# A recurrent layer on one core: small products outside the scan are held back behind the weight products

## The chip, the cores and the metric

One NeuronCore of a Trainium2 chip runs the whole layer. The metric is device time in microseconds (us) of one execution. The engines are PE (TensorE, matrix products), DVE (VectorE), ACT (ScalarE), POOL (GpSimd) and SP (which issues DMAs). Each works through its own instruction list in order and waits on semaphores for the others.

## The reference, cut to what matters

One layer with a context stream of 256 tokens and a latent stream of 256, width 2048. After a modulated norm, one input projection feeds two branches: 16 RWKV-7 heads and 4 gated linear attention heads.

```python
p = h @ lp["w_in"]
...
def step(s, inp):
    w_t, k_t, v_t, a_t, b_t = inp[:5]
    sa = jnp.einsum("bhvk,bhk->bhv", s, a_t)
    s = s * w_t[:, :, None, :] + sa[..., None] * b_t[:, :, None, :] + v_t[..., None] * k_t[:, :, None, :]
    y = jnp.einsum("bhvk,bhk->bhv", s, inp[5]) if emit else None
...
mixed = (jax.nn.sigmoid(f["g_a"]) * (y_a.astype(dt) @ lp["w_a"])
         + jax.nn.sigmoid(f["g_b"]) * (y_b.astype(dt) @ lp["w_b"]))
return mixed @ lp["w_out"]
```

The RWKV recurrence runs in both directions, over the context first and then over the latent tokens.

## The kernel before, in words

The kernel orders its own instructions. While the program is built, class `Issue` (from line 67) keeps a clock for each engine from estimated costs. Every piece of work is a generator, a track, which yields lists of operations; `run` (line 255) takes the track that can start first by these clocks, and `emit` (line 146) writes its operations to the engines. So the order on each engine is fixed once, and the chip follows it, however long things take there. In this text "planner" is this class, and "planned" times are its estimates.

A track has a number for its priority; the smaller one goes first among those that can start within 40 ns of each other. Track 99, `stream` (line 612), issues the **weight products**: 128x128 blocks of `w_in`, `w_a`, `w_b` and `w_out` against 256 tokens, each as three products (high and low halves, `three`, line 637). They fill `acc`. Before, ACT casts the raw weights to `wH` and DVE takes the difference `wL` (`splitter`, line 596); one such half tile serves 12 weight products, and five can be ready at a time.

The recurrent stretch (from line 1651) works through eight blocks of two heads. For each block these tracks run, and all but the last have priorities of 3 or more:

- `fe_track` (line 979): products `pq`, `pw`, `pal`, and on DVE the features `kn`, `C`, `bk`, `kd`, `ar`.
- `bt_track` (1093): transposes `pbt` of `bk`. `ab_track` (1105): products `pab`. `gg_track` (1119): `pgc`, `pgl`. `mv_track` (1238): transposes `pV`. `bv_track` (1068): `pb`.
- `inv_track` (1168): inverts 64x64 triangular blocks. ACT copies `Lin`, DVE transposes it to `M`, POOL runs a recurrence of 60 operations on `M` and `tm`, DVE transposes `M` back to `Lin`, then PE does `pH` and `pZ`, and ACT and DVE copy the result to `Z`.
- `sc_track` (1256), priority 2: **the scan**, eight steps of `p` (in the code `p1`), `pU`, `pSs` and `pY`, with copies on ACT and DVE between them, and after the last step `pyt`. It needs `Z`, `BK` and `UV` of its block.

During this stretch the weight products are those of 48 column blocks of `w_in` (`add_cm`, line 645); when the last block's features are made, those of `w_b` and `w_a` may follow. After the scans come the rest of these and `w_out`.

The choice of the next operation on PE in `run`, before:

```python
same = [x for w, x in c if x[6] == tr[6] and w <= w0 + win]
best = min(same, key=lambda x: x[0]() if callable(x[0]) else x[0])
if tr[6] == "pe" and self.since > 1200:
    best = next((x for x in same if x[0] == 99), best)
if tr[6] == "pe" and best[0] != 99 and 0.6 and self.cooling():
    best = next((x for w, x in c if x[0] == 99 and w <= w0 + 150), best)
```

Here `c` holds the tracks that could go and the time at which each could, `x[0]` is the priority, `x[3]` the list of operations, `x[5]` the planned time at which its inputs are there, and `win` is 40 ns. So a small product goes as soon as the planner holds it for ready, after the weight product in hand; the second rule lets a weight product in after 1200 ns of small ones, the third where the planner fears for the clock of PE.

Of the kernel before, what the change touches and what calls it, by code (L numbers as in the profile page):

```python
# [76 lines left out]
class Issue:  # L77
# [12 lines left out]
    def __init__(self, ps, groups):  # L90
        self.t = dict.fromkeys(self.LAT, 0.0)
        self.at, self.rd, self.rings, self.free_at, self.tracks = {}, {}, {}, {}, []
        self.ps, self.groups = ps, groups
        self.bank_free, self.bank_of = {b: 0.0 for g in groups.values() for b in g}, {}
        self.busy, self.psum, self.kept = set(), set(), {}
        self.n = 0
        self.table = 0
        self.work = self.since = self.small = 0.0
        self.load_at = self.stream_at = 0.0
        self.corners, self.ticks = [], {}  # L100

# [153 lines left out]
    def run(self, done):  # L255
        while not done():
            best, c = None, []
            for tr in self.tracks:
                w = self.when(tr)
                if w is None:  # L260
                    continue
                if w < 0:
                    best = tr
                    break
                c.append((w, tr))
            if best is None:
                if not c:
                    raise RuntimeError("stuck: " + str([(t[4], t[2].gi_frame.f_lineno) for t in self.tracks]))
                w0, tr = min(c, key=lambda x: x[0])
                win = 40  # L270
                same = [x for w, x in c if x[6] == tr[6] and w <= w0 + win]
                best = min(same, key=lambda x: x[0]() if callable(x[0]) else x[0])
                if tr[6] == "pe" and self.since > 1200:
                    best = next((x for x in same if x[0] == 99), best)
                if tr[6] == "pe" and best[0] != 99 and 0.6 and self.cooling():
                    best = next((x for w, x in c if x[0] == 99 and w <= w0 + 150), best)
            g = best[3]
            send = None
            if isinstance(g, list):
                w0 = self.work  # L280
                for op in g:
                    self.emit(op)
                if best[0] == 99:
                    self.since = 0.0
                else:
                    self.since += self.work - w0
                    self.small += self.work - w0
            elif isinstance(g, Claim):
                send = self.take(g)
            self.step(best, send)  # L290
# [40 lines left out]
def hybrid_layer(tc, a, out):  # L331
    nc = tc.nc
    es = ExitStack()
    with es:
# [6 lines left out]
        iss = Issue(ps, {"acc": (0, 1, 2, 3), "pa": (4, 5, 6, 7), "gg": (4, 5, 6, 7), "st": (2,), "u1": (3,), "py": (4,),  # L341
                         "g3": (5, 6, 7), "o2": (2, 3),
                         "f4": (0, 1, 2, 3, 4, 5, 6), "s1": (7,), "s2": (6, 7),
                         "xp": (0, 1, 2, 3, 4, 5, 6, 7)})
# [1304 lines left out]


        state["b0"] = iss.small
        iss.groups["acc"] = (0, 1)
        xes, fes = ExitStack(), ExitStack()
        xp = Pool(iss, xes.enter_context(tc.tile_pool(name="rwx", bufs=1, reuse_waits="tile")))
# [157 lines left out]
```

## Time and profile before

| | us |
|---|---|
| median of 3 runs | 1364.46 (1361.43 to 1368.26) |
| the profiled execution, own time | 1361.36 |
| its span, first to last instruction | 1359.6 |
| PE busy in it | 1270.1 (93%) |
| DVE busy | 968.3 (71%) |
| ACT busy | 718.2 (53%) |
| POOL busy | 543.3 (40%) |

The profile is of one execution. "Busy" counts an engine as busy while any instruction is in flight on it. An idle time in square brackets behind an instruction names the operation whose end it waited for. Nearly all instructions carry the line of one helper (L304 before), so they are told apart by the names of their tiles. The recurrent stretch lies at about 595 to 1125 us of the span, the last of the scan and its evacuation end near 1172, and the rest of the span is weight products.

### The profile page before, as it was taken

Reading aid. Unit: us, or ns where it says so; the run is one execution under the profiler, and the core shown is the slowest. Engines: PE = TensorE matmul, PEld = TensorE weight load, DVE = VectorE, ACT = ScalarE, POOL = GpSimd, SP = SyncE. Lnnn points to the kernel's source line nnn. Section 1 sums busy time; section 2 is a strip of 40 time slices with the busy share of each in tenths; the row PEclk is TensorE's granted clock in tenths of the full one; section 3 lists DMA queues with packets and bytes.
Section 4 is the critical chain, followed back from the end, with each engine's and each line's share of the span. In section 5 each row is a group of like instructions: output and inputs, shape, how many; then the busy total and the mean of one; then the engine's idle time right before and its main releaser. Section 6 shows DMA issues by size and latency. Waiting matters only on the chain. (4 is left out here: it accounts for less than half of the span.)

```text
span 1359.6 us, 29662 instructions
## 1 busy us (share of the span) xinstructions
PE 1270.1 (93%) x11479; PEld 1068.1 (79%) x11479; DVE 968.3 (71%) x2031; ACT 718.2 (53%) x1449; POOL 543.3 (40%) x684
## 2 busy tenths in 40 slices
PE   5999999999999999999899999799989999999996
PEld 3555578688788897998777778677878888999876
DVE  4433497885965737767978998698978776668656
ACT  5222244343334444486577678667766666445443
POOL 0000476676570000005888729673983550000012
PEclk9999999999999999999889999799979999999999
DMA  9999465455462433576632443234433545789564
GB/s 347 354 340 311 132 195 168 150 171 160 145 202 79 134 102 97 153 196 171 157 85 76 113 118 92 77 99 114 108 78 94 138 105 145 203 247 271 185 230 144
DMA packets 311186, 220.45 MB, mean 162 GB/s; under 512 B 37354, under 2 KB 286724, under 8 KB 310532
## 3 DMA queue, kind: packets, MB, share of 16 engines
q1 hardware_dynamic: 311044, 218.55, 55.5%
q8 instruction: 90, 1.47, 0.4%
q14 instruction: 52, 0.43, 0.1%
HBM read 199.76 MB, written 12.46 MB: 156 GB/s over the span
## 5 line engine op out<-in xcount | busy, mean ns | idle before, releaser
L304 DVE TENSOR_TENSOR wL<-raw,wH 128x512 fp32r<-128x512 f32 x484 | 377.2, 786 | 170.2 <-ACT wH L304 165.0
L304 ACT CAST wH<-raw 128x512 fp32r<-128x512 f32 x484 | 295.1, 616 | 328.5 <-PE acc L304 208.7
L304 PE MATMUL acc<-lH,wH 128*128 128x256 f32 x896 | 285.1, 318 | 0.5 <-ACT tg L304 0.5
L304 PE MATMUL acc<-lL,wH 128*128 128x256 f32 x896 | 256.0, 286 | 0.0
L304 PE MATMUL acc<-lH,wL 128*128 128x256 f32 x896 | 255.6, 285 | 0.2 <-DVE wL L304 0.2
L304 PEld LDWEIGHTS acc<-lH,wH 128*128 128x128 f32 x896 | 173.4, 194 | 21.1 <-issue 4.5
L304 POOL TENSOR_TENSOR tm<-M 64x30 f32<-64x30 f32 (+14 forms) x240 | 160.1, 667 | 74.3 <-DVE M L304 48.1
L304 POOL TENSOR_TENSOR M<-M,tm 64x30 f32<-64x30 f32 (+14 forms) x240 | 170.1, 709 | 18.7
L304 PEld LDWEIGHTS acc<-lL,wH 128*128 128x128 f32 x896 | 174.5, 195 | 3.1 <-issue 1.7
L304 PEld LDWEIGHTS acc<-lH,wL 128*128 128x128 f32 x896 | 173.9, 194 | 0.4 <-DVE wL L304 0.4
L304 PE MATMUL acc<-hH,wH 128*128 128x512 f32 (+1 forms) x416 | 168.7, 406 | 1.3 <-ACT lo L304 1.3
L304 PE MATMUL acc<-hH,wL 128*128 128x512 f32 (+1 forms) x416 | 157.2, 378 | 0.0
L304 PE MATMUL acc<-hL,wH 128*128 128x512 f32 (+1 forms) x416 | 156.3, 376 | 0.1
L304 PEld LDWEIGHTS acc<-hH,wH 128*128 128x128 f32 x416 | 78.6, 189 | 38.1 <-issue 22.9
L304 POOL TENSOR_TENSOR xs<-yg,fg 128x512 f32<-128x512 f32 (+1 forms) x10 | 13.5, 1371 | 231.4 <-DVE yg L304 231.4
L304 POOL TENSOR_TENSOR gw<-gw,csl 128x512 f32<-128x512 f32 x60 | 71.1, 1185 | 61.9 <-DMA gw<-in_w_mod_dram 61.9
L304 PEld LDWEIGHTS acc<-hH,wL 128*128 128x128 f32 x416 | 78.4, 188 | 15.5 <-DVE wL L304 0.4
L304 POOL TENSOR_TENSOR ga<-ga,gw 128x512 f32<-128x512 f32 x60 | 88.6, 1476 | 4.2
L304 PEld LDWEIGHTS acc<-hL,wH 128*128 128x128 f32 x416 | 78.9, 190 | 10.6 <-DVE hL L304 0.4
L304 PE MATMUL acc<-yH,wH 128*128 128x256 f32 x256 | 73.0, 285 | 0.0
L304 PE MATMUL acc<-yL,wH 128*128 128x256 f32 x256 | 72.8, 284 | 0.0
L304 PE MATMUL acc<-yH,wL 128*128 128x256 f32 x256 | 72.8, 284 | 0.0
(318 smaller groups left out, 2627.7 us busy)
## 6 DMA issues: line engine op xcount, KB each, us to landing
raw<-in_w_in_dram SPq DMA_DIRECT2D x174, 512.0 KB, 4.0
wm<-in_w_mod_dram SPq DMA_DIRECT2D x64, 512.0 KB, 6.9
gw<-in_w_mod_dram SPq DMA_DIRECT2D x64, 256.0 KB, 4.0
raw<-in_w_out_dram SPq DMA_DIRECT2D x32, 512.0 KB, 4.8
raw<-in_w_b_dram SPq DMA_DIRECT2D x16, 512.0 KB, 4.1
raw<-in_w_a_dram SPq DMA_DIRECT2D x16, 512.0 KB, 4.9
kv<-kvo SPq DMA_DIRECT2D x16, 256.0 KB, 3.9
tg<-tg SPq DMA_DIRECT2D x32, 128.0 KB, 3.8
```

Source lines behind the costliest of these rows:

```text
L304: op = Op("dma" if name == "dma_start" else self.key, name, lambda: f(*a, **k), aps[0], aps[1:], func, k.get("accum_out"), any(x.tensor.na ...
```

## The change

A list of small products of a track other than the scan is no longer taken if the last thing on PE was a weight product, a weight product is ready within 40 ns, and the list has been ready for less than 2000 planned ns. A weight product goes in its place, and the list is looked at again each time. The hold ends when the 2000 ns are over, when no weight product is ready, or when some other product, in practice one of the scan, has been taken: `on99` is then false and the held lists follow it freely. The hold is switched on at the start of the recurrent stretch.

```diff
@@ class Issue, __init__
+        self.defer, self.on99 = 0.0, False
@@ Issue.run
                 if tr[6] == "pe" and self.since > 1200:
                     best = next((x for x in same if x[0] == 99), best)
+                if (tr[6] == "pe" and self.defer and self.on99 and best[0] != 99 and isinstance(best[3], list)
+                        and (best[0]() if callable(best[0]) else best[0]) > 2 and self.t["pe"] - best[5] < self.defer):
+                    best = next((x for w, x in c if x[0] == 99 and isinstance(x[3], list) and w <= w0 + win), best)
...
                 for op in g:
                     self.emit(op)
+                if g[0].key == "pe":
+                    self.on99 = best[0] == 99
@@ the start of the recurrent stretch
         state["b0"] = iss.small
+        iss.defer = 2000.0
```

No operation is added or removed; the order on the engines is another from the first transposes `pV` of the stretch on. Three places follow. First PE in the second block, from `pw` to the transposes `pbt` of `bk`. Before:

```order
L304 MATMUL pw<-low,wh 128x512
L304 MATMUL pw<-low,wlo 128x512
L304 MATMUL acc<-lH,wH 128x256
L304 MATMUL acc<-lL,wH 128x256
L304 MATMUL acc<-lH,wL 128x256
L304 MATMUL pbt<-ident,bk 128x128 x4
L304 MATMUL pal<-low,wh 128x512
L304 MATMUL pal<-low,wlo 128x512
L304 MATMUL pbt<-ident,bk 128x128 x4
```

The same place in the changed program:

```order
L310 MATMUL pw<-low,wh 128x512
L310 MATMUL pw<-low,wlo 128x512
L310 MATMUL acc<-lH,wH 128x256
L310 MATMUL acc<-lL,wH 128x256
L310 MATMUL acc<-lH,wL 128x256
...
L310 MATMUL pbt<-ident,bk 128x128 x4
L310 MATMUL pal<-low,wh 128x512
L310 MATMUL pal<-low,wlo 128x512
L310 MATMUL pbt<-ident,bk 128x128 x4
```

The three rows of weight products stand there seven times in a row: 21 weight products instead of 3 ahead of `pbt`. From `pq` of this block to this `pbt` there were 105 weight products and are now 156.

Second DVE at the same place, where `bk` is made, from the copies `Dt` to the second `bk`. Before:

```order
L304 COPY Dt<-eC 128x4 x2
L304 SCALAR_TENSOR_TENSOR bk<-t_7006,C 128x8x64
L304 TENSOR_TENSOR wL<-raw,wH 128x512
L304 TENSOR_TENSOR kd<-kc,ta 128x512
L304 TENSOR_TENSOR wL<-raw,wH 128x512
L304 SCALAR_TENSOR_TENSOR rc<-acc,vec,rc 128x3x63
L304 TENSOR_TENSOR bk<-kd,C 128x8x64
```

In the changed program:

```order
L310 COPY Dt<-eC 128x4 x2
L310 TENSOR_TENSOR wL<-raw,wH 128x512
L310 SCALAR_TENSOR_TENSOR rc<-acc,vec,rc 128x3x63
L310 SCALAR_TENSOR_TENSOR bk<-t_7123,C 128x8x64
L310 TENSOR_TENSOR wL<-raw,wH 128x512
L310 SCALAR_TENSOR_TENSOR rc<-acc,vec,rc 128x4x63
L310 TENSOR_TENSOR kd<-kc,ta 128x512
L310 TENSOR_TENSOR wL<-raw,wH 128x512
L310 SCALAR_TENSOR_TENSOR rc<-acc,vec,rc 128x4x63
L310 TENSOR_TENSOR wL<-raw,wH 128x512
L310 SCALAR_TENSOR_TENSOR rc<-acc,vec,rc 128x3x63
L310 TENSOR_TENSOR bk<-kd,C 128x8x64
```

From `kn` of this block to this second `bk` there were 6 splits `wL` and one operation on `rc`, and are now 9 and 6. Ahead of the first scan step as a whole DVE has 9 splits more than before.

Third PE at `pH` of the fourth block, which stands among the scan steps of the third. Before:

```order
L304 MATMUL pab<-ar,bk 64x64 x16
L304 MATMUL acc<-lH,wH 128x256
L304 MATMUL acc<-lL,wH 128x256
L304 MATMUL acc<-lH,wL 128x256
L304 MATMUL pSs<-UV,BK 64x64 x4
L304 MATMUL pY<-UV,GMr 64x64 x4
L304 MATMUL pH<-Lin,GMo 32x32 x16
```

In the changed program:

```order
L310 MATMUL acc<-lH,wH 128x256
L310 MATMUL acc<-lL,wH 128x256
L310 MATMUL acc<-lH,wL 128x256
...
L310 MATMUL pSs<-UV,BK 64x64 x4
L310 MATMUL pY<-UV,GMr 64x64 x4
L310 MATMUL pH<-Lin,GMo 32x32 x16
```

The weight products ahead of `pSs` stand there seven times again, 21 instead of 3, and `pab` of the next block has moved behind `pH`.

Over the whole program from the stretch on, PE's 3369 weight products lay in 266 unbroken runs and lie in 255 now. Up to the first scan step there were 573 of them and are 669 now; up to the last `pSs` 2073, now 2217; after it 1296, now 1152.

## Rows read from the trace of the kernel before

**Rows 1.** The page, engines: busy us, share of the span, instructions.

```profile
PE 1270.1 (93%) x11479; PEld 1068.1 (79%) x11479; DVE 968.3 (71%) x2031; ACT 718.2 (53%) x1449; POOL 543.3 (40%) x684
```

**Rows 2.** Stages: window and length, busy us (instructions) by engine, PE's clock, DMA.

```profile
595.00:1175.00 580.00, 536.69 (x6591) 466.24 (x6591) 472.10 (x999) 397.04 (x838) 346.91 (x509) 0.95 0.44 114
1175.00:1360.00 185.00, 172.01 (x1163) 158.59 (x1161) 121.85 (x216) 84.04 (x158) 13.54 (x10) 0.98 0.70 217
```

**Rows 3.** Waits of PE, 595 to 1175 us: total us, times, longest.

```profile
PE pH L304 <- DVE Lin L304: 9.6, 4, 6.9
PE p L304 <- DVE UV L304: 6.0, 13, 1.9
PE pSs L304 <- DVE UV L304: 3.9, 9, 1.0
PE pbt L304 <- DVE bk L304: 3.5, 1, 3.5
PE pbt L304 <- ACT BK L304: 3.0, 1, 3.0
...
PE pgl L304 <- ACT rs L304: 2.4, 1, 2.4
...
PE pq L304 <- ACT sz L304: 1.8, 1, 1.8
PE pgl L304 <- DVE Z L304: 1.8, 1, 1.8
PE pgl L304 <- DVE GMr L304: 1.4, 1, 1.4
...
PE pgl L304 <- DVE GM L304: 0.7, 1, 0.7
```

**Rows 4.** The chain that ended last: start us, length, what.

```profile
1172.27 84.60 PE acc L304 x705
```

**Rows 5.** Timeline of PE around `pab` of the first block: start us, length, instruction.

```profile
616.01 0.28 PE L304 MATMUL acc<-lH,wL 128*128 128x256 f32 x1
616.22 1.15 PE L304 MATMUL pab<-ar,bk 64*64 64x64 f32 x32
617.30 0.39 PE L304 MATMUL acc<-lH,wH 128*128 128x256 f32 x1
617.52 0.28 PE L304 MATMUL acc<-lL,wH 128*128 128x256 f32 x1
```

**Rows 6.** Timeline of DVE and PE at `pbt` of the second block.

```profile
645.35 1.15 DVE L304 TENSOR_TENSOR wL<-raw,wH 128x512 fp32r<-128x512 f32 x1
...
650.77 0.40 DVE L304 SCALAR_TENSOR_TENSOR rc<-acc,vec,rc 128x189 f32<-128x189 f32 x1
651.10 0.77 DVE L304 TENSOR_TENSOR bk<-kd,C 128x512 f32<-128x512 f32 x1
...
651.92 1.12 PE L304 MATMUL pbt<-ident,bk 128*128 128x128 f32 x4 [3.46 <-DVE bk L304]
```

**Rows 7.** Timeline of POOL and DVE ahead of `pH` of the fourth block.

```profile
857.31 0.25 POOL L304 TENSOR_TENSOR M<-M,tm 64x30 f32<-64x30 f32 x1
...
857.68 2.03 DVE L304 STREAM_TRANSPOSE Lin<-M 64x1024 f32<-64x1024 f32 x1 [5.61 <-POOL M L304]
```

**Rows 8.** Stages: POOL's recurrence of the first and of the last block.

```profile
625.50:674.30 48.80, 43.22 (x366) 40.83 (x367) 42.42 (x66) 28.16 (x48) 44.11 (x62) 0.93 0.58 151
1065.00:1107.70 42.70, 41.37 (x463) 35.65 (x463) 32.33 (x79) 26.19 (x70) 37.96 (x61) 1.00 0.56 143
```

**Rows 9.** Timeline of PE and DVE from `pZ` to `Z`, first block.

```profile
683.15 1.53 PE L304 MATMUL pZ<-Lin,GMo 32*32 32x32 f32 x48
...
687.93 0.69 DVE L304 COPY Z<-pZ 32x512 f32<-32x512 f32 x1 [0.65 <-ACT Z L304]
```

**Rows 10.** Timeline of PE just after the wait of rows 6.

```profile
654.76 0.41 PE L304 MATMUL acc<-lL,wH 128*128 128x256 f32 x1
654.97 0.41 PE L304 MATMUL acc<-lH,wL 128*128 128x256 f32 x1
```

**Rows 11.** The page, costliest groups: the split of the weights.

```profile
L304 DVE TENSOR_TENSOR wL<-raw,wH 128x512 fp32r<-128x512 f32 x484 | 377.2, 786 | 170.2 <-ACT wH L304 165.0
```

## The prediction

> **What bounds the kernel now.** I read the page's engine busy times first, then two stages, then PE's waits in the first stage, then the timeline at single places. PE is busy for 93% of the span [rows 1]: of 1359.6 us it lacks 89.5. Nearly half of that lies in the recurrent stretch: of its 580 us PE is busy for 536.7, so 43.3 us are idle [rows 2]. After it PE has weight products alone: 705 of them in 84.60 us, 0.12 us each, without a break [rows 4]. So the program ends when PE has done all its products, and a weight product that moves from the tail into the stretch changes nothing by itself. What can change the time is idle time of PE, the number of times that it changes between kinds of products, and its clock.
>
> The waits of the stretch name the idle time [rows 3]. Two of the ten rows belong to the scan (`p` and `pSs` for `UV`, 9.9 us), which the change does not hold. The other eight stand ahead of products that can be held: `pH` 9.6 us, `pbt` 3.5 and 3.0, `pgl` 2.4, 1.8, 1.4 and 0.7, `pq` 1.8, **24.2 us** in all. At these places the planner thought an input ready that came later, and everything behind it on PE, weight products too, stood still. The reader should see in [rows 6, 7] why: `pbt` waited 3.46 us for `bk`, which stood on DVE behind a 1.15 us split and an `rc` operation, and `pH` waited for `Lin`, the last link of a chain through POOL's recurrence. DVE is busy for 472.1 of the 580 us [rows 2], so it is the engine behind most of these waits.
>
> **The change part by part.** It adds no operation. It moves 96 weight products (11.5 us at 0.12) ahead of the first scan step and takes 144 (17.3 us) from behind the last `pSs`. Both are PE time at either place, so they cancel; the sum is made of the following.
>
> *Waits ahead of held products.* A hold of 2.0 planned us gives an input up to 2.0 us more. Were each wait shortened by that, `pH` would give 2.0 of its longest and all of its other 2.7, `pbt` 2.0 twice, `pgl` 5.9, `pq` 1.8: 16.4 us, the upper end. The lower end is nothing, because a weight product put ahead on PE also puts its split ahead on DVE. At the second block's `pbt` this can be counted. From `pq` to there PE has 51 weight products more, 6.1 us. From `kn` to `bk` DVE has 3 splits and 5 `rc` operations more; at 1.15 and 0.40 us, the lengths just there [rows 6], that is 5.5 us. The wait of 3.46 us shrinks by 0.6 only. At `pH` of the first block there are 48 weight products more since `pab` (5.8 us), but the 32 `pab` of the next block have moved behind it (two groups of 1.08 us from start to start [rows 5]) and three run edges are gone (0.6): 3.0 us more cover. The four splits among them cost DVE 3.1 us at the mean of 0.786 [rows 11]. POOL's recurrence took 48.8 us with DVE busy for 42.4, and 42.7 us with DVE busy for 32.3 [rows 8], 0.6 us for each us of DVE: 1.9 us longer. I take the difference, 1.1 us. At `pH` of the fourth block, the longest wait, 18 weight products more stand just ahead (2.2 us), but only 3 more over the whole chain since its `pab` (0.4); I take 1.3, the middle. For the rest (`pbt` 3.0, `pgl` 6.3, `pq` 1.8) I can't count both sides; the hold can give 9.7 at most, and I take half, 4.9, since their inputs lie nearer to PE than the long chains of the two counted places. Together **7.9 us**.
>
> *New waits.* In the second block `pU` follows `pZ` closely now: six weight products in two runs (1.1 us), `pb`, `p` and one group of `pgl`, some 3.0 us as an estimate from their like in [rows 5]. From the end of `pZ` to the end of `Z` took 3.9 us (684.7 to 688.6) [rows 9]. That makes a wait of 0.9. In the fifth and seventh blocks the chain from `pab` to `pH` is covered by 21 and 18 weight products fewer, 4.7 us; before, these two hardly waited, so some slack is there, and I take about half, 2.5. Bounds: nothing, and 5.6. Together 3.4, so the waits give 7.9 - 3.4 = **4.5 us** net.
>
> *Changes between kinds.* A run of weight products costs more than its 0.12 each: from its last start to the next small product 0.21 us, and from its first to its second start 0.22 [rows 5], so 0.19 more a run. Eleven runs fewer (255 for 266): **2.1 us**. This is certain to within its own size.
>
> *Clock.* The granted clock of the stretch is 0.95 [rows 2], so about 58 us of it (an estimate; the rounding allows 52 to 64) ran at 1.2 instead of 2.4 GHz. Such a dip follows a standstill: after the 3.46 us wait weight products start every 0.21 us instead of 0.12 [rows 10]. A net 4.5 of 43.3 us idle is 10%; 10% of the dips is 6 us at the lower level, worth between 0 and 3; I take **1.5 us**, because in a dip the chains on DVE and POOL go on as before.
>
> The page "TensorE: Matmul & The Clock Gate" of the Trainium skill (section Terms) puts the penalty at the throttled time times one minus the ratio of the clocks, half of it here; by that the term would be 2.9 us and the sum 9.5. The step of 0.21 against 0.12 us agrees for weight products; for the small ones no run here shows it.
>
> *Other queues.* SP issues the raw weights earlier, ahead of some small loads of the blocks. No wait of rows 3 was ended by a DMA, so I cost that at nothing; what hides it are the weight tiles that are loaded ahead. If that cover went, a scan would wait for its `GM` copies, and rival B would be nearer.
>
> Sum: 4.5 + 2.1 + 1.5 = 8.1 us off the profiled execution's 1361.36 gives 1353.3. The median of the runs shown, 1364.46, is 3.1 us above that execution, so I forecast **1356.4 us**.
>
> **The rivals.** *A, the waits move on with the splits.* The second block's `pbt` is then typical: 0.6 of 3.5 us, 17%. Of 24.2 us go 4.1, less 3.4 of new waits, plus 2.1 for the runs: 2.8 us, 1361.7 on the median's scale. For it speaks DVE's load, against it that half of the waits are under 2 us.
>
> *B, slower: DVE is the bound ahead of the first scan.* DVE has 9 splits more there. At 1.15 us each [rows 6] they cost 10.4 us, and POOL's recurrences beside them 6.2 (0.6 each us [rows 8]), 16.6 in all, against 11.5 us of weight products done early: 5.1 lost. The new waits come at their full 5.6, and dips in proportion (10.7 of 43.3 is 25% of 58, 14 us at the lower level, half of at most 7 us: 3.6). Less 2.1 for the runs that is 12.2 us more: 1376.7. It decides when the added DVE work exceeds what DVE has free; in the first recurrence that is 48.8 - 42.4 = 6.4 us [rows 8], which speaks against the full price. For it speaks that a split took 1.15 us beside the recurrence against 0.786 in the mean [rows 6, 11]. The Trainium skill ("GPSIMD Engine Reference", Specifications) says that POOL shares its SBUF interfaces with DVE and contends with DVE instructions that have two SBUF inputs, as a split has; by that rule every split moved beside a recurrence slows both, and B is the outcome. The longer split and the longer recurrence agree with it.
>
> *C, the hold works in full.* Every held wait loses its 2.0 us: 16.4, plus 2.1, plus dips in proportion (38% of 58 us, 22 at the lower level, at most 11, half 5.5): 24.0 us, 1340.5. Against it stands the count at the second block's `pbt`.
>
> That the change does nothing is no rival: the order on PE differs as shown.
>
> **How the numbers follow.** About 0.5% (6.8 us) is what a measurement of this kernel can tell from no change, so "faster" is below 1357.6 and "slower" above 1371.3. The forecast gets 0.45; its own range, from the bounds of its terms, is 1349 to 1363, and since its middle lies just below the border I count 0.31 of it as faster, 0.14 as the same. A gets 0.18, the same. B gets 0.22, of which 0.20 slower and 0.02 the same, since its price can come in part. C gets 0.15, faster. That makes 0.46 faster, 0.34 the same, 0.20 slower. The range reaches from near C to near B, 1342 to 1374, and leaves out half of each.
>
> **What would show it right or wrong.** PE's idle time in the recurrent stretch should be some 39 us instead of 43.3, at a clock of 0.95 or a little above. Right: the `pgl` and `pq` waits are mostly gone, the `pbt` wait in the second block is near 2.9 us, the `pH` wait in the fourth 5 to 6; the first scan step starts some 10 us later, and the unbroken weight products of the tail are fewer. Wrong in A's way: the sum of the held waits stays near 24. Wrong in B's way: the first scan starts over 15 us later, the recurrences take over 50 us, `pU`, `pSs` and `pH` wait longer, and the clock is 0.93 or less. Wrong in C's way: idle time under 30 us.

## The result, and the profile after

The changed kernel took **1377.16 us** in the median of five runs (1374.91 to 1378.17), the kernel before 1363.71 in five runs beside them: a ratio of 1.0091, 95% interval 1.0065 to 1.0117. The forecast was 1356.4 with a range of 1342 to 1374. The sign is wrong and the range does not hold the time. Slower by over 0.5% had a chance of 0.20, and the rival that had it, B, named another place and another mechanism; that its 1376.7 us lies 0.5 us from the measured time is luck.

The engines of the page of the profile after, span 1374.1 us, beside [rows 1]:

```profile
PE 1272.8 (93%) x11479; PEld 1070.8 (78%) x11479; DVE 975.2 (71%) x2031; ACT 716.0 (52%) x1449; POOL 540.4 (39%) x684
```

The span is 14.5 us longer. PE's busy time is 2.7 of that; the other 11.8 are idle time of PE (1374.1 - 1272.8 = 101.3, against 89.5). The same two stages as in [rows 2], cut 15 us later because the scan ends later:

```profile
595.00:1190.00 595.00, 540.63 (x6604) 470.40 (x6603) 480.92 (x984) 396.78 (x837) 343.94 (x509) 0.95 0.43 114
1190.00:1375.00 185.00, 171.40 (x1154) 157.52 (x1153) 122.67 (x232) 83.78 (x160) 13.52 (x10) 0.98 0.68 209
```

In the recurrent stretch PE is idle for 54.4 us (595.0 - 540.63) instead of 43.3: 11.1 of the 11.8. The tail is as before, and the clock has the same 0.95. So the question is what PE waits for in the stretch. Its waits there (total us, times, longest), to be laid beside [rows 3]:

```profile
PE p L310 <- DVE UV L310: 12.6, 18, 2.1
PE pSs L310 <- DVE UV L310: 8.1, 11, 1.7
PE pSs L310 <- ACT UV L310: 4.7, 5, 2.8
PE pyt L310 <- DVE xc L310: 3.9, 2, 3.2
PE pyt L310 <- ACT BK L310: 3.9, 2, 2.1
PE pH L310 <- DVE Lin L310: 3.6, 3, 2.0
PE pbt L310 <- DVE bk L310: 2.8, 1, 2.8
PE p L310 <- issue: 2.0, 3, 1.1
PE pU L310 <- ACT R L310: 1.8, 2, 1.3
PE pgl L310 <- DVE GMr L310: 1.4, 1, 1.4
```

The list is turned round. Before, the longest entry was `pH` for `Lin`, 9.6 us with a longest of 6.9; now it is 3.6 with a longest of 2.0, and of the five `pgl` and `pq` entries in [rows 3] one is left among these rows. In their place stand the scan's own products: `p` for DVE's `UV` went from 6.0 to 12.6 us, `pSs` for it from 3.9 to 8.1, and `pSs` for ACT's `UV` and `pyt` are new among the large ones. Summed over all waits by the product that waited, held products lost 25.0 us before and 12.7 after; the scan's products (`p`, `pU`, `pSs`, and `pyt` behind them) 16.7 before and 40.1 after.

One such new wait, in the timeline of all engines in the sixth block (start us, length, engine, instruction, idle time before it and what ended that):

```profile
1075.92 4.38 ACT L310 COPY Lin<-AB 32x512 f32<-32x512 f32 x4 [0.24 <-DVE AB L310]
...
1076.80 0.45 PE L310 MATMUL pSs<-UV,BK 128*64 128x64 f32 x8
...
1077.56 0.46 DVE L310 SCALAR_TENSOR_TENSOR Sn<-pSs,Dt,SD 128x64 f32<-128x64 f32 x2
...
1080.33 1.24 DVE L310 STREAM_TRANSPOSE M<-Lin 64x1024 f32<-64x1024 f32 x1 [2.31 <-ACT Lin L310]
...
1081.59 0.29 ACT L310 COPY UV<-Sn 64x128 f32<-64x128 f32 x1
...
1081.61 0.22 DVE L310 COPY UV<-Sn 64x128 f32<-64x128 f32 x1
...
1081.97 0.45 PE L310 MATMUL p<-UV,GM 128*64 128x64 f32 x8 [1.95 <-DVE UV L310]
```

Read it from below. The scan step `p` waited 1.95 us for the copies `UV<-Sn`, of which DVE makes one half and ACT the other. `Sn` had been done at 1078.0, but on DVE the transpose `M<-Lin` of the eighth block stands ahead of the copy, and it was idle for 2.31 us until ACT had finished four copies `Lin<-AB`. On ACT the copy of the scan stands behind the same four, and behind two more of that chain, so it came no earlier. The scan, which goes first in the planner, was late because of a chain that goes after it. At 814.96 us, in the second block, the same pattern cost `p` another 2.15 us.

Before the change, the copies of the eighth block fell into the scan of the sixth block too:

```profile
1058.91 2.18 ACT L304 COPY Lin<-AB 32x512 f32<-32x512 f32 x2 [0.76 <-DVE AB L304]
1059.89 0.22 DVE L304 COPY UV<-Sn 64x128 f32<-64x128 f32 x1
...
1061.12 0.29 ACT L304 COPY UV<-Sn 64x128 f32<-64x128 f32 x1
1061.44 2.15 ACT L304 COPY Lin<-AB 32x512 f32<-32x512 f32 x2
1061.47 0.45 PE L304 MATMUL p<-UV,GM 128*64 128x64 f32 x6 [0.69 <-ACT UV L304]
1063.63 1.24 DVE L304 STREAM_TRANSPOSE M<-Lin 64x1024 f32<-64x1024 f32 x1 [2.20 <-ACT Lin L304]
```

There the scan's copy stood between two and two of them on ACT and ahead of the transpose on DVE, and `p` waited 0.69 us. The transpose waited for ACT before the change as well: over the eight blocks 13.1 us before and 16.4 after. What is new is what stands behind it.

The planner's formula gives an ACT copy `Lin<-AB` 94 + 0.833 x 512 = 521 ns; here four took 4.38 us, 1.10 each, and they took as long before the change (32 of them, mean 1.09).

### The profile page after: what moved, and what is told of

Read it like the earlier page. It is cut to its first block, busy times and chain, and to the rows that moved or that the text cites. A ratio compares the mean times of both kernels' runs of the same rounds, so it can differ in the third digit from the quotient of the medians.

```text
span 1374.1 us, 29653 instructions
## 1 busy us (share of the span) xinstructions
PE 1272.8 (93%) x11479; PEld 1070.8 (78%) x11479; DVE 975.2 (71%) x2031; ACT 716.0 (52%) x1449; POOL 540.4 (39%) x684
## 4 chain that ended last, share of the span: by engine, by line
PE 60%; DVE 20%; POOL 5%; issue 5%; ACT 4%; DMA 4%; SPq 1%; DVEq 0%; ACTq 0%; POOLq 0%
PE acc L310 37%; DVE wL L310 6%; PE pv L310 5%; PE pout L310 3%; PE pg L310 3%; POOL tm L310 2%; POOL M L310 2%; ACT Lin L310 2%; PE pS L310 1%; ACT wH L310 1%; DMA raw<-in_w_out_dram 1%; PE pSs L310 1%; DVE UV L310 1%; PE p L310 1%; DVE kvo L310 1%
## 5 line engine op out<-in xcount | busy, mean ns | idle before, releaser
L310 PEld LDWEIGHTS acc<-lH,wH 128*128 128x128 f32 x896 | 174.6, 195 | 20.1 <-issue 4.3
L310 POOL TENSOR_TENSOR M<-M,tm 64x30 f32<-64x30 f32 (+14 forms) x240 | 166.5, 694 | 18.7
L310 POOL TENSOR_TENSOR xs<-yg,fg 128x512 f32<-128x512 f32 (+1 forms) x10 | 13.5, 1368 | 229.2 <-DVE yg L310 229.2
L310 PEld LDWEIGHTS acc<-hL,wH 128*128 128x128 f32 x416 | 78.9, 190 | 10.7 <-DVE hL L310 0.4
L310 POOL TENSOR_TENSOR ga<-ga,gw 128x512 f32<-128x512 f32 x60 | 84.7, 1411 | 4.2
```

Source lines behind the costliest of these rows:

```text
L310: op = Op("dma" if name == "dma_start" else self.key, name, lambda: f(*a, **k), aps[0], aps[1:], func, k.get("accum_out"), any(x.tensor.na ...
```

## Experiments

Each was timed beside the kernel before on the same chip. "No hold" means that the change's rule is left out. "Held" and "scan" in the tables are sums of PE's waits in the stretch as above, `pyt` counted with the scan, from one profile each.

### A re-ordered program without the hold

The first theory, Chain in the expectations, was that the hold delays the hand-offs from one block to the next scan; its rival, Luck, that any other order costs as much. Luck is tried by a setting that has nothing to do with the hold: the 40 ns within which priorities decide become 36 or 50 from the start of the stretch on. The order then differs from there.

```diff
-                win = 40
+                win = self.win
...
         state["b0"] = iss.small
+        iss.win = 36
```

> The kernel before with no hold, but with 36 instead of 40 planned ns as the window in which the planner prefers the smaller priority, from the start of the recurrent stretch on. It has no purpose but to give another order of the same operations. Theory Chain (the hold delays each hand-off of the chain from one block's features to its Z, so that the next scan starts late): no hold, so within 0.3% of before, 1360 to 1368 us. Theory Luck (the order before fits the chip unusually well, and any other order of this planner is slower): 0.5 to 1.2% slower, 1371 to 1380 us. In the order the weight products between the end of a scan and the start of the next are 285, against 171 before and 282 in the changed kernel; by Luck this is what counts, and the time comes near 1377.

> As the run with 36 ns, with 50 planned ns. Chain: within 0.3% of before, 1360 to 1368 us. Luck: slower, but by less than with 36 ns, since 219 weight products lie between the scans: 0.2 to 0.7%, 1366 to 1373 us.

Measured: 1.0086 [1.0053, 1.0119] and 1.0110 [1.0053, 1.0168]. A change of 4 planned ns, without any hold, costs what the change cost, and Chain's range is missed twice. Luck's own refinement, that the number of weight products between the scans sets the time, fails too: e2 has fewer of them than e1 and is not faster, and e12 below, with the most (366), was expected over 1380 us and took 1372.4. Three more widths, of which the 44 leaves the order as it was until the third block's scan:

> The kernel before without hold, window 44 planned ns from the stretch on. Its order is that of before up to the scan of the third block and another after it. Luck (any other order of this planner loses): slower, but less than with 36 or 50 ns, since the first part is kept: 0.3 to 0.8%, 1369 to 1376 us. Hold (the loss is the hold's own, and the two other windows were bad by accident): within 0.3% of before, 1361 to 1369 us.

> The kernel before without hold, window 60 planned ns from the stretch on. Both theories now (the hold gains on an ordinary order; the order before is unusually good): 0.7 to 1.2% slower than before, 1374 to 1382 us. If the gain of the hold was an accident of three windows, this one may lie anywhere from 1365 to 1382.

> The kernel before without hold, window 30 planned ns. As with 60: 0.7 to 1.2% slower than before, 1374 to 1382 us.

Measured: 1.0082 [1.0052, 1.0111], 1.0122 [1.0088, 1.0156] and 1.0112 [1.0081, 1.0144]. So the order before is not one of many alike: all five neighbours tried lose 0.8 to 1.2%, some 11 to 17 us.

### The hold on a part of the tracks

e3 holds only the lists of the side tracks (`gg`, `mv`, `bt`, `bv`), e4 only those of the chain (`fe`, `ab`, `inv`).

```diff
-                if (tr[6] == "pe" and self.defer and self.on99 and best[0] != 99 and isinstance(best[3], list)
+                if (tr[6] == "pe" and self.defer and self.on99 and best[4][:2] in ("gg", "mv", "bt", "bv") and best[0] != 99 and isinstance(best[3], list)
```

> The changed kernel with the hold only for tracks beside the serial chain: gg, mv, bt and bv (pgc, pgl, pV, pbt, pb). Chain: the chain is not held, so the loss goes, 1360 to 1366 us; some waits ahead of pgl and pbt go as well. Luck: another order again, 195 weight products between the scans, 0.1 to 0.6% slower than before, 1365 to 1372 us.

> The changed kernel with the hold only for the tracks of the serial chain: fe, ab and inv (pq, pw, pal, pab, pH, pZ). Chain: the whole loss or more, 1374 to 1385 us, with the time from the last step of one scan to the first of the next longer by 20 us or more in all than before. Luck: slower too, in the range of the runs with another window (336 weight products between the scans), so this run alone does not tell the two apart; beside the run that holds the others it does.

Measured: 1.0043 [1.0020, 1.0065] for the side tracks, 1.0117 [1.0085, 1.0149] for the chain. It looks as if holding the chain were what hurts (waits of the scan 20.9 and 34.3 us; the held waits did not fall, 27.6 and 25.4). But both times lie within what orders without a hold show, so this alone settles nothing. Chain's own sign, longer gaps from the last `p` of one scan to the first of the next, came true in e4: 136.5 us in sum against 96.1 before. But it does not set the time, since PE does weight products in these gaps: they sum to 127.8 us in the changed kernel and 127.2 in e1, but to 94.9 in e5, which was 0.8% slower, and to 159.4 in e17 below, which was 0.3% slower.

### The hold against no hold, at the same setting

The proper comparison is a pair: the same window, with and without the hold.

```diff
         state["b0"] = iss.small
+        iss.win = 44
         iss.defer = 2000.0
```

> The changed kernel, window 44 planned ns. Beside the run with the same window and no hold this shows what the hold does to an order that was not the one of before. Luck: the two differ by less than 0.4% either way, 1370 to 1381 us. Hold: 0.7 to 1.2% slower than the same window without hold.

> The changed kernel, window 50 planned ns; the same window without hold took 1378.0 us. Luck: 1372 to 1384 us, on either side of that. Hold: 1388 to 1394 us, 0.7 to 1.2% above it.

> The changed kernel, window 36 planned ns; the same window without hold took 1375.4 us. Luck: 1369 to 1381 us, on either side of that. Hold: 1385 to 1392 us.

> The changed kernel, window 60 planned ns. If the hold gains on an ordinary order, 0.2 to 1.1% faster than the same window without hold, 1362 to 1376 us, with waits ahead of held products of 10 to 14 us instead of 19 to 25. If that was an accident: as often slower as faster.

> The changed kernel, window 30 planned ns. If the hold gains on an ordinary order, 0.2 to 1.1% faster than the same window without hold. In its order 366 weight products lie between the scans, the most of all; if that number set the time, it would be the slowest, over 1380 us.

All five medians came out below their partner without the hold, at window 36 within the noise; e6 and e7 were faster than either theory had allowed. A rule seemed near: the hold gains on an ordinary order and loses only on the well-fitting one before. To test it on orders made in another way, the planner's latency from a PE product to its use was set to 190 and 210 ns instead of 200:

```diff
         state["b0"] = iss.small
+        iss.LAT = dict(iss.LAT, pe=190.0)
```

> The kernel before without hold, window 40 planned ns as before, but 190 instead of 200 planned ns from a product of PE to its use, from the stretch on. If the order before is unusually good in general: 0.7 to 1.2% slower, 1374 to 1381 us. If only the window of 40 matters: within 0.3% of before, 1361 to 1369 us.

> The changed kernel with 190 planned ns from PE to use. If the hold gains on an ordinary order: 0.2 to 1.2% faster than the same without hold; waits ahead of held products 10 to 15 us instead of 19 to 27, waits of the scan 33 to 40 instead of 24 to 31.

> The kernel before without hold, 210 instead of 200 planned ns from PE to use, window 40. As with 190: 0.7 to 1.2% slower than before, or within 0.3% if only the window matters.

> The changed kernel with 210 planned ns from PE to use. If the hold gains on an ordinary order: 0.2 to 1.2% faster than the same without hold. If the changed kernel's own time shows what the hold does: 0.9% slower than the same without hold.

The rule fell: with 190 the hold lost 1.0%, with 210 it made no clear difference. Without the hold both were slower than before by 0.9 and 1.4%, so the window of 40 is not what is special.

### Costs that the planner has too low

The theory here was that the waits ahead of held products exist because the planner gives some operations too little time. For POOL's recurrence its formula gives 27.6 us in sum (60 operations: 30 at 149 + 1.667 n and 30 at 149 + 2.096 n ns, the n adding up to 4960 each), where [rows 8] show 48.8 and 42.7. A split is planned at 68 + 1.042 x 512 = 602 ns and takes 786 [rows 11]. The last pair raises both, without and with the hold:

```diff
+        if Op.late and key == "pool" and name == "tensor_tensor":
+            c *= 1.55
+        if Op.late and key == "dve" and name in ("tensor_tensor", "tensor_sub") and n == 512 and not psum:
+            c += 185
         self.cost = c
...
         state["b0"] = iss.small
+        Op.late = True
```

> No hold; instead two costs of the planner are raised to what the traces show, from the stretch on: POOL's tensor_tensor times 1.55 (its sixty operations of one recurrence are planned at 27.6 us, the trace of before shows 42.7 and 48.8), and 0.185 us more for a DVE tensor_tensor of 512 columns (a split then 0.786 us, as in the trace). Theory 'the waits ahead of the held products come from costs planned too low': the waits of pH, pbt and the other held products fall from 25 us to under 15 with no hold at all, the scan's stay near 20 us, and the time is 0.995 to 1.003 of before. Rival 'any order other than that before gives up its fit': the waits move elsewhere and the ratio is 1.008 to 1.014, as in the seven re-orderings without the hold.

> The change (hold of 2000) with the two costs raised as in e17_true. Theory 'the hold only makes up for costs planned too low': with them raised it has nothing left to give, and the time is 0.000 to 0.008 above that of e17_true, the scan's waits rising to 30 to 40 us as in every order with the hold. Rival 'the hold has a gain of its own': 0.003 to 0.010 below e17_true. By the scatter of the pairs so far (hold against no hold from -1.2% to +1.0%) only a difference beyond that would speak clearly.

All nine pairs, the change itself first (ratio to before; us of waits and the mean granted clock of the runs as a share of full speed, no hold -> hold):

| setting | no hold | with hold | hold, % | held | scan | clock |
|---|---|---|---|---|---|---|
| as before | 1 | 1.0091 [1.0065, 1.0117] | +0.9 | 25.0 -> 12.7 | 16.7 -> 40.1 | 0.975 -> 0.973 |
| window 30 | 1.0112 [1.0081, 1.0144] | 1.0054 [1.0038, 1.0071] | -0.6 | 24.5 -> 14.0 | 27.2 -> 36.4 | 0.968 -> 0.978 |
| window 36 | 1.0086 [1.0053, 1.0119] | 1.0069 [1.0041, 1.0097] | -0.2 | 18.9 -> 13.5 | 27.6 -> 40.0 | 0.974 -> 0.976 |
| window 44 | 1.0082 [1.0052, 1.0111] | 1.0031 [1.0011, 1.0051] | -0.5 | 25.3 -> 10.7 | 23.9 -> 37.4 | 0.974 -> 0.977 |
| window 50 | 1.0110 [1.0053, 1.0168] | 1.0001 [0.9981, 1.0021] | -1.1 | 20.1 -> 13.8 | 30.6 -> 35.0 | 0.975 -> 0.980 |
| window 60 | 1.0122 [1.0088, 1.0156] | 1.0006 [0.9986, 1.0026] | -1.1 | 26.6 -> 14.4 | 26.1 -> 32.7 | 0.970 -> 0.977 |
| latency 190 | 1.0091 [1.0049, 1.0133] | 1.0187 [1.0152, 1.0222] | +1.0 | 35.1 -> 18.3 | 21.7 -> 29.0 | 0.977 -> 0.963 |
| latency 210 | 1.0137 [1.0090, 1.0183] | 1.0152 [1.0120, 1.0184] | +0.1 | 20.4 -> 16.4 | 29.8 -> 35.2 | 0.972 -> 0.969 |
| costs raised | 1.0026 [1.0004, 1.0049] | 1.0156 [1.0118, 1.0194] | +1.3 | 19.1 -> 20.2 | 31.4 -> 37.6 | 0.969 -> 0.957 |

Three things follow. **First**, the hold moves waits, it does not remove them: over the nine pairs the held products' waits fall by 9.0 us in the mean, in eight of them, and the scan's rise by 9.8, in every pair. **Second**, its effect on the time has no sign of its own: the nine differences run from -1.1 to +1.3% with a mean of 0.0; at window 36 and latency 210 the intervals overlap. **Third**, the order before is a rare one: its scan waits, 16.7 us, are the lowest of all twenty programs (next the side tracks' 20.9, at 1.0043). No version beat it; windows 50 and 60 with the hold equal it within the noise.

The waits of window 50, without and with the hold, show the exchange on an order other than that before. Without (e2):

```profile
PE pH L305 <- DVE Lin L305: 9.4, 5, 4.5
PE p L305 <- DVE UV L305: 9.0, 13, 2.0
PE pSs L305 <- DVE UV L305: 5.0, 7, 1.5
PE pbt L305 <- DVE bk L305: 4.6, 2, 3.5
```

With (e7):

```profile
PE p L311 <- DVE UV L311: 9.1, 18, 1.1
PE pSs L311 <- DVE UV L311: 9.1, 12, 1.5
PE pSs L311 <- ACT UV L311: 5.9, 5, 2.1
PE pH L311 <- DVE Lin L311: 3.0, 4, 1.4
PE pbt L311 <- DVE bk L311: 2.8, 1, 2.8
```

`pH` gives back 6.4 us and `pbt` 1.8, `pSs` takes 4.1 for DVE's `UV` and waits up to 2.1 us for ACT's. Yet this pair gained 1.1%: the sums of waits in the stretch do not account for a difference of that size.

The pages of the profiles tell more. The span of e2 is 1377.5 us, of which PE is busy for 1275.4 and idle for 102.1; of e7 it is 1365.8, busy 1269.3 and idle 96.5. So 6.1 of the 11.7 us lie in PE's busy time, for the same 11479 products, and the mean granted clock is 0.974 against 0.981. Where the hold lost, at latency 190, it is plainer. The stretch without and with the hold (e13, then e14; columns as in [rows 2]):

```profile
595.00:1210.00 615.00, 556.86 (x6766) 486.85 (x6766) 489.07 (x1019) 406.84 (x854) 350.33 (x509) 0.96 0.44 116
```

```profile
595.00:1210.00 615.00, 563.83 (x6709) 490.00 (x6708) 492.95 (x1011) 407.82 (x856) 344.77 (x509) 0.93 0.43 113
```

With the hold PE is idle for 7.0 us less there, at a lower clock. Over the whole program its idle time falls from 104.6 to 97.9 us and its busy time rises from 1272.0 to 1291.9. In all nine pairs the version with the lower mean clock is the slower one. So a part of the differences goes with the clock that an order is granted; whether the clock causes it, and why one order is granted less, no run shows.

The last pair was to part "the waits come from costs planned too low" from "any other order loses". It did not: 1.0026 is better than every other re-ordering without the hold, but `pH`, `pbt` and the rest still waited 19.1 us, where under 15 were expected, and the scan 31.4, where about 20 were. With the hold it lost 1.3%, and its profile shows a loss of another kind. Windows of e18 late in the stretch (columns as in [rows 2]):

```profile
1040.00:1080.00 40.00, 28.68 (x304) 23.04 (x304) 30.44 (x60) 22.14 (x43) 33.51 (x57) 0.66 0.17 44
1080.00:1120.00 40.00, 31.17 (x419) 25.36 (x417) 25.16 (x61) 22.30 (x52) 16.25 (x35) 0.65 0.12 29
1120.00:1160.00 40.00, 27.58 (x268) 23.87 (x269) 23.59 (x50) 16.55 (x39) 17.28 (x32) 0.67 0.51 142
```

PE is idle for 32.6 of these 120 us, the granted clock is about two thirds of 2.4 GHz, so some two thirds of the time it was at 1.2, and until 1120 us the DMA moves only 44 and 29 GB/s. A likely reason is in the groups by line for the same 120 us. In e18, then in the kernel before:

```profile
L315 PE MATMUL acc<-lH,wH 128*128 128x256 f32 x34 | 14.5, 427 | 0.0
...
L315 PE MATMUL acc<-yH,wH 128*128 128x256 f32 x17 | 5.3, 313 | 0.0
```

```profile
L304 PE MATMUL acc<-lH,wH 128*128 128x256 f32 x155 | 50.6, 326 | 0.0
```

Of each of the three kinds of weight product there are 51 (34 on `w_in`, 17 on the weights that follow) instead of 155, and between 1080 and 1120 us next to none. Those on `w_in` had been used up earlier: from 1080 us on 16 of each kind were left, against 130 before the change. So the end of the sixth scan and the gap before the seventh had nothing to fill PE, and in the seventh `pU` once waited 8.1 us for ACT's `R`. The change itself does not run dry so: it has 133 of that kind in the same window and 107 left at 1080 us. But e17, without the hold, does too, if less: 24 were left, and PE is idle for 21.1 of the same 120 us. So the last pair tells little of the hold, and e17 is not a clean test of the costs.

## Why the prediction was wrong

**The step that failed** is the one ahead of the sum: "Two of the ten rows belong to the scan (`p` and `pSs` for `UV`, 9.9 us), which the change does not hold. The other eight stand ahead of products that can be held". The scan's waits for its own copies entered the sum with nothing. They and `pyt` rose by 23.4 us (16.7 to 40.1), more than everything the forecast wanted to gain. That the scan is not held was true and beside the point: what is held is its neighbours, and with them moves all that DVE and ACT do for them, in order, between the scan's own copies. The timeline at 1075.92 shows such a place, and 814.96 is another, 1.95 and 2.15 us; that all of the 23.4 came about in this way is not shown, and the re-orderings without the hold raise the scan's waits too, to between 21.7 and 31.4. The terms of new waits looked at `pU` behind `pZ` and at `pH` in the fifth and seventh blocks (3.4 us), which is a seventh of what came; the scan's steps were not looked at.

**The second failure** is one of the base. The working took the order before for an ordinary one, whose waits could only be helped. The eight re-orderings without the hold, 0.3 to 1.4% slower, show that each of the eight other orders gave up some 4 to 19 us. No rival stood for that. The profile of one kernel can't show it; a rival with less trust in a sum of 8 us could have stood for it.

**What held waits gave** was more than forecast. They fell by 12.3 us; the forecast was 7.9 before the new waits are taken off, with 16.4 as the upper end. The counted place came out as counted: the second block's `pbt`, 3.46 us [rows 6], predicted near 2.9:

```profile
674.19 1.05 PE L310 MATMUL pbt<-ident,bk 128*128 128x128 f32 x4 [2.84 <-DVE bk L310]
```

At `pH` of the fourth block, predicted 5 to 6, more was gained: no `pH` wait is over 2.0.

**Rival B's place is refuted.** The first `p` came at 693.4 us instead of 686.0, 7.4 us later, though 96 weight products more (11.5 us) stand ahead of it; B wanted over 15. The first recurrence started 7.2 us later (632.81 us instead of 625.57) and did not get longer. Its sixtieth operation ends at 681.51 us in the changed kernel and at 674.12 before: 48.70 us against 48.55. All eight took 371.7 us in sum, 372.5 before; since the longest took 50.8 us now and 51.5 before, B's sign of over 50 could tell nothing. The window that belongs to [rows 8], first block (columns as in [rows 2]):

```profile
632.74:681.54 48.80, 43.95 (x342) 42.46 (x343) 41.70 (x63) 30.05 (x53) 44.10 (x61) 0.97 0.58 156
```

DVE is busy for 41.70 us of it instead of 42.42 [rows 8], with 23 splits in either: the splits that B counted beside it did not fall there. Its price of 1.15 us for one was high too: the 23 took 21.0 us before, 0.91 each. So this place did not put to the test the rule of the Trainium skill on which B leaned ("GPSIMD Engine Reference", Specifications: POOL contends for SBUF with DVE instructions that have two SBUF inputs); no run here shows it for or against.

**Where the time went** is the scan part. From the first `p` to the last `pSs` it took 471.2 us before (686.0 to 1157.2) and 493.9 after (693.4 to 1187.3), 22.7 more, of which 48 weight products more are 5.8. The eight scans themselves, from first to last `p`, take 363.1 us in sum instead of 372.2; the gaps between them grew by 31.7, and PE filled these in part with weight products. The tail behind it got shorter by 15.6 us (202.4 to 186.8; 17.3 were reckoned), as forecast. Together 7.4 + 22.7 - 15.6 is the 14.5 us of the span.

**Changes between kinds**, "certain to within its own size" at 2.1 us gained, cannot be seen: PE's busy time rose by 2.7.

**Clock.** Forecast 1.5 us gained. The stretch shows 0.95 as before. In the 75 runs of the kernel before beside the experiments, the nine with a mean clock of 0.980 or more took 1357.2 to 1363.5 us and the six with 0.967 or less 1369.8 to 1371.5; a line through all 75 gives 6.8 us for 0.01 of the clock. The five runs of the change have 0.973 in the mean, before 0.975: by that line some 1.6 us of the 13.5 lost. For e18, at 0.957, it would be some 13 of its 20.8. The Trainium skill ("TensorE: Matmul & The Clock Gate", Terms) counts half of the throttled time as lost; as an estimate by that, 0.01 of 1362 us is 27.2 us at the lower level and 13.6 lost. These runs show half of it, as the forecast's term assumed; since this is a correlation between runs, it does not show the cause.

**What stays open.** Why the order before has the lowest scan waits, and why the same exchange of waits comes with a higher clock and 1.1% gained at one window, with a lower clock and 1.0% lost at another latency. An obvious next repair was not tried: ACT's copies `Lin<-AB`, planned at 0.52 us and measured at 1.10, which stood ahead of the scan's copy in the timeline shown.

## What to carry to other kernels

Where a planner fixes the order of in-order engines, a rule that delays some work can move all that serves this work on the other engines too; list the waits of the work that is *not* touched and cost them as well. Before crediting or blaming a rule, re-order the same program by something that should not matter (here 4 planned ns) and see how far the time moves; here that was 1%, as much as the rule. And a hold that spends filler early must be checked against the filler's supply at the end.

## What the runs showed of the hardware that was not expected

Idle time of PE did not cost clock in proportion: the stretch of the change has 11.1 us more of it (54.4 for 43.3) at the same granted 0.95, and the stretch of e14 has 7.0 us less than that of e13 (51.2 for 58.1) at 0.93 instead of 0.96. Where PE was idle for 32.6 of 120 us (e18), the clock fell to 0.65 to 0.67. And of the executions of one and the same program, those with the higher clock were up to 14.3 us faster (1357.2 to 1371.5 in the 75 runs of the kernel before), as much as the change moved the median.
